# Forgetting attention in a hybrid decoder step: query tiles taken in pairs, the value products of a pair alternating between the two column halves of TensorE

## The chip, the cores and the metric

One NeuronCore of a Trainium2 chip runs one launch of the kernel. The metric is the device time of that launch in microseconds (us). A profiled execution of the kernel before is on hand with its own time beside the span that the profile shows.

## What is computed

The reference is one inference step of a hybrid decoder layer: a combined input projection of 1024 prompt tokens and 32 sample tokens, four parallel head groups (gated DeltaNet, Mamba-2 SSD, forgetting attention "FoX", cross-attention into a memory), an output projection and a LayerNorm. The change is in FoX for the prompt: 8 heads of width 64, 1024 queries and keys, causal, with a cumulative log-forget bias `c`:

```
s = einsum('bqhd,bkhd->bhqk', q, k) * FOX_DH ** -0.5
s = s + cq[..., :, None] - ck[..., None, :]
s = where(k_pos[None, :] <= q_pos[:, None], s, -1e30)
p = softmax(s, axis=-1)
o = einsum('bhqk,bkhd->bqhd', p, v)          # then y_c = o * silu(c_gate)
```

## The kernel before, in words

The kernel is written against a tile framework. Its author writes operations in program order, and a scheduler sets at build time the order in which each engine gets them; on the chip every engine works through its own list in that order and waits on semaphores. So an edit of one function moves instructions of others too, and the order on an engine is read from the built program.

FoX runs in `fox(hp)`, once for each pair of heads hp = 0..3, and in it for both heads of the pair (h2 = 0, 1). A head's queries are cut into eight tiles of 128 (qt = 0..7). Query tile qt needs the keys of blocks 0..qt, in at most two chunks of 512 keys (i = 0, 1). For each chunk:

- scores: matmuls of q1 with k1 and with k2 into a PSUM tile `fs` (lines 586 and 587), a mask matmul on the last block (589), then VectorE adds the bias row `cB`, writes `S` and keeps the row minimum `mn` (590, 593);
- ScalarE takes the exponential in place and sums it into `rs` (597);
- TensorE transposes `S` block by block into the PSUM tile `ft` (helper line 219), ScalarE and VectorE in turn copy it to `P` in SBUF (214, 216);
- value products: for each block of 128 keys one matmul with the value block `vt[:, kt, 64 columns]` as weights and the block of `P` as moving data, accumulated over the blocks in the PSUM tile `fo` (line 605). A value block has 64 columns, so the product fills 64 of the array's 128 columns; `o[64 * h2:64 * h2 + 64]` puts all products of one head into the same column half.

Line 609 multiplies the result into the gate tile `g2`. After both heads the row sums are inverted, transposed (`fr`, `rr`), multiplied in and written to DRAM. A head has 36 key blocks, so all eight heads have 288 value products. Each is fp32 and shows as two records on TensorE, 576 in all.

The tile `vt` (the values of a head pair, 512 KB) is loaded by SyncE's queue (SP) at line 568, two buffers deep; `k1`, `k2`, `q1`, `cB` come by GpSimd's queue (lines 561, 563, 495). SP's queue is in order too: a load that waits for its buffer holds those behind it. `fs` has two PSUM banks, `ft` (shared with `fr`) one, `fo` one.

`run()` weaves the 64 steps of `fox` with 37 steps of the DeltaNet recurrence `gdn()`; the scheduler fills in matmuls of the last input projections (`pj`, line 356) and, once these are used up, of cross-attention (`cs`, `cT`, `co`, `cr`) and of the sample tokens (`zs`, `zo`). Later the SSD part (`by`, line 1372) runs with the output projection (`op`, line 1557). Line 1372 also has weights of 64 columns, and its products go to the two column halves in turn by twos:

```
q, c = 64 * (k % 2), 128 * (k // 2)
nc.tensor.matmul(Y[g][q:q + 64, c:c + 128], lhsT=xdt[:, 4 * g + k, :], rhs=E[:, 4 * g + k, :],
                 start=(k < 2), stop=(n == 0 and k > 1), tile_position=(0, q))
```

Of the kernel before, what the change touches and what calls it, by code (L numbers as in the profile page):

```python
# [10 lines left out]
F32 = mybir.dt.float32  # L11
# [4 lines left out]
AF = mybir.ActivationFunctionType  # L16
ALU = mybir.AluOpType
# [153 lines left out]
class K:  # L171
# [373 lines left out]
    def fox(self, hp):  # L545


        nc, fx = self.nc, self.fx
        vt = fx.tile([128, 8, 128], F32, tag="vt", name="vt", bufs=2)
        g2 = fx.tile([128, T], F32, tag="g2", name="g2", bufs=2)  # L550
# [5 lines left out]
        for h2 in range(2):  # L556
# [16 lines left out]
            for qt in range(8):  # L573
                n = 128 * (qt + 1)
                ch = [(c, min(n, c + 512)) for c in range(0, n, 512)]
                mn = fx.tile([128, 2], F32, tag="mn", name="mn", bufs=3)
                Ss = []
                for i, (c0, c1) in enumerate(ch):
                    p = self.g("fs")
                    S = fx.tile([128, 512], F32, tag="S", name="S", bufs=3)  # L580
                    Ss.append(S)
                    w = c1 - c0

                    w2 = max(w, 256)
                    last = c1 == n
                    nc.tensor.matmul(p[:, :w2], lhsT=q1[:, qt * 128:n], rhs=k1[:, c0:c0 + w2], start=True, stop=False)  # L586
                    nc.tensor.matmul(p[:, :w2], lhsT=q1[:, qt * 128:n], rhs=k2[:, c0:c0 + w2], start=False, stop=not last)  # L587
                    if last:
                        nc.tensor.matmul(p[:, w - 128:w], lhsT=self.identb, rhs=self.foxm, start=False, stop=True)
                    nc.vector.tensor_tensor_reduce(out=S[:, :w], in0=p[:, :w], in1=cB[:, c0:c1], op0=ALU.add, op1=ALU.min,  # L590
                                                   scale=1.0, scalar=3e38, accum_out=mn[:, i:i + 1])
                if len(ch) == 2:
                    nc.vector.tensor_tensor(out=mn[:, 0:1], in0=mn[:, 0:1], in1=mn[:, 1:2], op=ALU.min)
                o = self.g("fo")
                for i, (c0, c1) in enumerate(ch):
                    S, w = Ss[i], c1 - c0
                    nc.scalar.activation(out=S[:, :w], in_=S[:, :w], func=AF.Exp, scale=-1.0, bias=mn[:, 0:1], accum_out=rs[:, qt, h2, i:i + 1])  # L597
# [9 lines left out]
                s = slice(qt * 128, n)  # L607
# [8 lines left out]
        for a in range(2):  # L616
            p = self.g("fr")
            rr = fx.tile([128, 512], F32, tag="S", name="rr", bufs=3)
# [1000 lines left out]
    def run(self):  # L1619
# [4 lines left out]
        with ExitStack() as self.ctx_x:  # L1624
# [46 lines left out]
            t = self.fx.tile([128, 512], F32, tag="P", name="constF", bufs=2)[:, 0:128]  # L1671
# [120 lines left out]
```

## Time and profile before

| | |
|---|---|
| median of 3 runs | 1478.03 us (1476.21 to 1480.02) |
| profiled execution: its own time | 1479.97 us |
| profiled execution: span of the profile | 1478.1 us |
| TensorE (PE) matmul busy | 1373.3 us, 93% |
| PE weight loads (PEld) busy | 1140.2 us, 77% |
| VectorE (DVE) / ScalarE (ACT) / GpSimd (POOL) busy | 829.6 / 499.3 / 440.3 us |
| mean granted TensorE clock | 0.972 of full speed |
| first and last value product of FoX start at | 834.0 and 1186.8 us |

The span runs from the first to the last instruction; the execution's own time is 1.9 us longer. "Busy" of PE counts a matmul from its start to a modelled end, and matmuls are pipelined, so the step from one start to the next says more of its price than its duration. Names such as `fo<-P,vt` read "written tile <- read tiles".

### The profile page before, as it was taken

What the parts mean: (1) busy time and instruction counts of PE and PEld (TensorE: products, weight loads), DVE (VectorE), ACT (ScalarE), POOL (GpSimd) and SP (SyncE); (2) the same over time, 40 slices, a digit from 0 to 9 for tenths busy, and PEclk for the clock granted to TensorE, in tenths of its full rate; (3) what the DMA queues carried; (4) which work ended last, traced back from release to release, by engine and by line L of the source; (5) the groups of instructions that cost most, each with busy time, mean ns of one, the idle gap of its engine ahead of it and who ended that gap; (6) DMA issues with size and microseconds to landing.
All of it is one profiled execution on the core that took longest, in us unless ns stands there. A gap on an engine that the chain in (4) does not pass through costs nothing.

```text
span 1478.1 us, 30323 instructions
## 1 busy us (share of the span) xinstructions
PE 1373.3 (93%) x11222; PEld 1140.2 (77%) x11222; DVE 829.6 (56%) x2149; ACT 499.3 (34%) x1288; POOL 440.3 (30%) x465
## 2 busy tenths in 40 slices
PE   8999999999989998999998899999899978999996
PEld 6898888987777887888887788777676655676764
DVE  4524223364766757452355545777575655866488
ACT  4422222243424343322332333554443320313132
POOL 1445322233524443332201101110120043344446
PEclk9999999999999999999999999999999988999998
DMA  6559898877778886988768444656547465463322
GB/s 241 195 197 377 311 324 312 311 268 272 246 261 299 277 295 234 319 308 298 285 220 209 144 117 119 220 183 178 169 126 212 166 203 191 105 201 89 125 65 106
DMA packets 184477, 324.30 MB, mean 219 GB/s; under 512 B 47177, under 2 KB 110954, under 8 KB 184330
## 3 DMA queue, kind: packets, MB, share of 16 engines
q1 hardware_dynamic: 113744, 241.39, 48.1%
q10 hardware_dynamic: 41930, 59.11, 11.3%
q0 software_dynamic: 28656, 21.88, 5.9%
q8 instruction: 88, 1.44, 0.4%
q14 instruction: 59, 0.48, 0.1%
HBM read 262.23 MB, written 60.01 MB: 218 GB/s over the span
## 4 chain that ended last, share of the span: by engine, by line
PE 42%; DMA 10%; DVE 5%; issue 4%; POOL 2%; ACT 1%; ACTq 0%; SPq 0%; DVEq 0%; POOLq 0%
PE pj L356 13%; PE op L1557 6%; PE fo L605 4%; PE ft L219 2%; PE dA L701 1%; PE fs L586 1%; PE dO L720 1%; DMA bE<-gS 1%; PE co L817 1%; PE fs L587 1%; PE cs L802 1%; DMA ggB<-gS 1%; DMA pg<-in_cache 1%; DMA mr<-mixD 1%; DMA qd<-aD3qd 1%
## 5 line engine op out<-in xcount | busy, mean ns | idle before, releaser
L356 PE MATMUL pj<-xh,wh 128*128 128x352 f32 x1152 | 383.8, 334 | 15.8 <-ACT u L214 8.8
L356 PE MATMUL pj<-xh,wl 128*128 128x352 f32 x1152 | 381.0, 331 | 3.8 <-DVE wl L342 3.8
L356 PE MATMUL pj<-xl,wh 128*128 128x352 f32 x1152 | 380.8, 331 | 0.0
L356 PEld LDWEIGHTS pj<-xh,wh 128*128 128x128 f32 x1152 | 220.4, 192 | 30.5 <-ACT u L214 10.3
L356 PEld LDWEIGHTS pj<-xh,wl 128*128 128x128 f32 x1152 | 221.0, 192 | 11.8 <-issue 6.5
L356 PEld LDWEIGHTS pj<-xl,wh 128*128 128x128 f32 x1152 | 220.4, 191 | 10.7 <-issue 10.0
L1557 PE MATMUL op<-wo,mh 128*128 128x512 f32 x512 | 165.9, 404 | 7.3 <-DVE acc L1563 4.2
L342 POOL TENSOR_TENSOR wl<-wr,wh 128x1024 fp32r<-128x1024 f32 x41 | 97.8, 2386 | 106.5 <-ACT wh L341 101.5
L655 POOL DMA_INDIRECT lf<-in_logf,ix x64 | 68.7, 1073 | 202.5 <-DVE cb L658 151.1
L725 DVE SCALAR_TENSOR_TENSOR Oacc<-Oacc,dmb,dO 128x512 f32<-128x512 f32 x64 | 47.6, 743 | 140.7 <-PE dO L720 132.5
L1557 PEld LDWEIGHTS op<-wo,mh 128*128 128x128 f32 x512 | 97.7, 194 | 37.0 <-issue 8.1
L1557 PE MATMUL op<-wo,ml 128*128 128x512 f32 x256 | 102.9, 404 | 3.2 <-POOL ml L1529 3.1
L900 DVE SCALAR_TENSOR_TENSOR y<-u,cw,y 128x1080 f32<-128x1080 f32 x54 | 79.8, 1477 | 22.7 <-ACT y L898 22.3
L701 PEld LDWEIGHTS dA<-pg,QD 128*32 128x32 f32 x2048 | 60.6, 110 | 40.4 <-issue 27.1
L605 PE MATMUL fo<-P,vt 128*64 128x128 f32 x576 | 83.9, 282 | 6.5 <-DVE P L216 5.6
L701 PE MATMUL dA<-pg,QD 128*32 128x128 f32 x2048 | 81.6, 277 | 8.0 <-DMA pg<-in_cache 4.6
L597 ACT ACTIVATE S<-S,mn 128x512 f32<-128x512 f32 (+2 forms) x96 | 58.6, 611 | 56.5 <-DVE mn L590 35.2
L605 PEld LDWEIGHTS fo<-P,vt 128*64 128x64 f32 x576 | 60.6, 137 | 20.5 <-DVE P L216 7.9
L720 PE MATMUL dO<-pg,dP 128*32 128x512 f32 x512 | 71.0, 598 | 4.7 <-ACT dP L717 4.7
L563 POOL DMA_DIRECT2D k<-kD x16 | 13.2, 837 | 180.1 <-PE fs L587 114.1
L709 ACT ACTIVATE dmb<-dmb 128x1 f32<-128x1 f32 x64 | 18.8, 293 | 130.0 <-DVE dmb L708 113.0
L1557 PEld LDWEIGHTS op<-wo,ml 128*128 128x128 f32 x256 | 49.3, 193 | 17.0 <-POOL ml L1529 4.0
(521 smaller groups left out, 2476.0 us busy)
## 6 DMA issues: line engine op xcount, KB each, us to landing
pg<-in_cache SPq DMA_DIRECT2D x256, 512.0 KB
wr<-in_w_in SPq DMA_DIRECT2D x48, 512.0 KB
k<-kD POOLq DMA_DIRECT2D x16, 512.0 KB, 19.4
wq<-in_w_out SPq DMA_DIRECT2D x16, 512.0 KB
mr<-mixD SPq DMA_DIRECT2D x32, 256.0 KB
xr<-in_xT SPq DMA_DIRECT2D x8, 528.0 KB
gateD<-gt ACTq DMA_DIRECT2D x24, 176.0 KB
mrow<-in_w_mem SPq DMA_DIRECT2D x8, 512.0 KB
```

Of the source, the lines that this page charges most:

```text
L219: self.nc.tensor.transpose(out, in_, self.c("ident", n)[:, :n])
L342: (eng or self.se).tensor_tensor(out=l, in0=r, in1=h.bitcast(F32), op=ALU.subtract)
L356: nc.tensor.matmul(ps[:n], lhsT=w[:, k, :], rhs=x[:, k, s], start=(k == 0 and q == 0), stop=(k == KD - 1 and q == 2))
L597: nc.scalar.activation(out=S[:, :w], in_=S[:, :w], func=AF.Exp, scale=-1.0, bias=mn[:, 0:1], accum_out=rs[:, qt, h2, i:i + 1])
L605: nc.tensor.matmul(o[64 * h2:64 * h2 + 64, 0:128], lhsT=vt[:, kt, 64 * h2:64 * h2 + 64], rhs=P[:, b4 * 128:(b4 + 1) * 128], start=(kt == 0 ...
L655: nc.gpsimd.indirect_dma_start(out=lf, out_offset=None, in_=I["logf"], in_offset=bass.IndirectOffsetOnAxis(ap=ix[:, j:j + 1].bitcast(U32), ...
L701: nc.tensor.matmul(ps[32 * b:32 * b + 32, 0:n], lhsT=QD[:, 4 * gr + b, hp, :], rhs=key(hp, b), start=(hp == 0), stop=(hp == 3), tile_posit ...
L709: nc.scalar.activation(out=mb[:, 1:2], in_=m, func=AF.Exp, scale=-1.0, bias=mb[:, 0:1])
L720: nc.tensor.matmul(po[32 * b:32 * b + 32, :], lhsT=P[:n, 32 * b:32 * b + 32], rhs=value(b), start=True, stop=True, tile_position=(0, 32 * b))
L725: nc.vector.scalar_tensor_tensor(out=O_, in0=O_, scalar=mb[:, 1:2], in1=po, op0=ALU.mult, op1=ALU.add)
L900: nc.vector.scalar_tensor_tensor(out=y, in0=u[:, i:i + CWD], scalar=w[:, i:i + 1], in1=y, op0=ALU.mult, op1=ALU.add)
L1557: nc.tensor.matmul(p[:m], lhsT=l[:, k, :], rhs=W[k][0][:, w, s], start=(k == 0 and q == 0), stop=(k == kn - 1 and q == 2))
```

## The change

Query tiles are taken two at a time, pair (2m, 2m + 1), m = 0..3. The scores, minima and exponentials of both tiles are issued first; then the generator yields, so that the woven parts may come in between; then for each key chunk the transposes and copies of both tiles, and the value products of both. The even tile of the pair goes to column half 0 of one `fo` tile, the odd one to half 1, whatever the head, with an explicit `tile_position`, and block by block the two alternate, odd tile first. Where both tiles' blocks of a chunk number four or fewer, they share one `ft` bank and one copy. Every product of a chunk is issued behind its first one, so a chunk's products start only when both copies are there. Line 609's multiply now reads the half of the tile and writes the half of the head. Buffers: `vt` 2 to 1, `S` 3 to 4, `P` 2 to 3, `mn` 3 to 4.

```diff
-        vt = fx.tile([128, 8, 128], F32, tag="vt", name="vt", bufs=2)
+        vt = fx.tile([128, 8, 128], F32, tag="vt", name="vt", bufs=1)
...
-            for qt in range(8):
...
-                for i, (c0, c1) in enumerate(ch):
-                    S, w = Ss[i], c1 - c0
-                    nc.scalar.activation(out=S[:, :w], ..., accum_out=rs[:, qt, h2, i:i + 1])
-                    P = fx.tile([128, 512], F32, tag="P", name="P", bufs=2)
-                    p = self.g("ft")
-                    for b4 in range(w // 128):
-                        self.tr(p[:, b4 * 128:(b4 + 1) * 128], S[:, b4 * 128:(b4 + 1) * 128])
-                    self.copy(P[:, :w], p[:, :w])
-                    for b4 in range(w // 128):
-                        kt = c0 // 128 + b4
-                        nc.tensor.matmul(o[64 * h2:64 * h2 + 64, 0:128], lhsT=vt[:, kt, 64 * h2:64 * h2 + 64],
-                                         rhs=P[:, b4 * 128:(b4 + 1) * 128], start=(kt == 0), stop=(kt == qt))
+            for m in range(4):
+                pair = (2 * m, 2 * m + 1)
+                mns, Ss = {}, {}
+                for qt in pair:
...
+                    for i, (c0, c1) in enumerate(ch):
+                        S, w = Ss[qt, i], c1 - c0
+                        nc.scalar.activation(out=S[:, :w], ..., accum_out=rs[:, qt, h2, i:i + 1])
+                yield
                 o = self.g("fo")
+                for i in range(len(ch)):
+                    nb = {qt: min(4, qt + 1 - 4 * i) for qt in pair}
+                    P, first = {}, None
+                    for qs in (pair,) if sum(nb.values()) <= 4 else (pair[:1], pair[1:]):
+                        blk = [(qt, b4) for qt in qs for b4 in range(nb[qt])]
+                        Pt = fx.tile([128, 512], F32, tag="P", name="P", bufs=3)
+                        p = self.g("ft")
+                        for j, (qt, b4) in enumerate(blk):
+                            self.tr(p[:, j * 128:(j + 1) * 128], Ss[qt, i][:, b4 * 128:(b4 + 1) * 128])
+                            P[qt, b4] = Pt[:, j * 128:(j + 1) * 128]
+                        self.copy(Pt[:, :128 * len(blk)], p[:, :128 * len(blk)])
+                    for b4 in range(nb[pair[1]]):
+                        kt = 4 * i + b4
+                        for half in (1, 0):
+                            qt = pair[half]
+                            if b4 >= nb[qt]:
+                                continue
+                            with self.tc.issue_after(first.ins) if first else nullcontext():
+                                d = nc.tensor.matmul(o[64 * half:64 * half + 64, 0:128], lhsT=vt[:, kt, 64 * h2:64 * h2 + 64],
+                                                     rhs=P[qt, b4], start=(kt == 0), stop=(kt == qt), tile_position=(0, 64 * half))
+                            first = first or d
-                nc.vector.tensor_tensor(out=g2[r, s], in0=o[r, 0:128], in1=g2[r, s], op=ALU.mult)
+                for half, qt in enumerate(pair):
+                    s = slice(qt * 128, qt * 128 + 128)
+                    nc.vector.tensor_tensor(out=g2[r, s], in0=o[64 * half:64 * half + 64, 0:128], in1=g2[r, s], op=ALU.mult)
                 yield
```

How the built order moves is shown at three places. The first is TensorE's list in the first head, query tiles 2 and 3. Before, each tile's products (`fo`, line 605) stand behind its own transposes:

```order
L219 MATMUL ft_11572<-constG_250,S_11564 128x128 x3
L586 MATMUL fs_11664<-k1_11451,q1_11450 128x512
L587 MATMUL fs_11664<-k2_11452,q1_11450 128x512
L586 MATMUL fs_11669<-k1_11451,q1_11450 128x256
L587 MATMUL fs_11669<-k2_11452,q1_11450 128x256
L589 LDWEIGHTS identb_11220
L589 MATMUL fs_11669<-foxm_11219,identb_11220 128x128
L605 MATMUL fo_11569<-P_11571,vt_11448 64x128 x3
L219 MATMUL ft_11591<-constG_250,S_11583 128x128 x4
L605 MATMUL fo_11588<-P_11590,vt_11448 64x128 x4
```

In the change the same two tiles' seven products stand in one run (now line 620), behind score matmuls of the fourth pair:

```order
L588 MATMUL fs_11787<-k1_11451,q1_11450 128x384
L589 MATMUL fs_11787<-k2_11452,q1_11450 128x384
L591 LDWEIGHTS identb_11220
L591 MATMUL fs_11787<-foxm_11219,identb_11220 128x128
L620 MATMUL fo_11574<-P_11581,vt_11448 64x128
L620 MATMUL fo_11574<-P_11575,vt_11448 64x128
L620 MATMUL fo_11574<-P_11581,vt_11448 64x128
L620 MATMUL fo_11574<-P_11575,vt_11448 64x128
L620 MATMUL fo_11574<-P_11581,vt_11448 64x128
L620 MATMUL fo_11574<-P_11575,vt_11448 64x128
L620 MATMUL fo_11574<-P_11581,vt_11448 64x128
L219 MATMUL ft_11657<-constG_250,S_11627 128x128 x4
```

`P_11581` is the odd tile's copy and `P_11575` the even one's: the two groups became one that alternates. Over all heads the 288 products stand in 96 unbroken groups before and in 52 in the change.

The second place is SP's list at the load of the second head pair's values (`vt<-vD1`). Before, it stands right behind the first loads of the stage:

```order
L568 DMA vt_11448<-vD0_79 128x1024
L569 DMA g2_11449<-gateD8_128 128x1024
L1040 DMA qd_11514<-aD0qd_97 128x512
L1040 DMA Kt_11516<-aD0Kt_99 128x512
L1040 DMA QK_11518<-aD0QK_96 128x512
L568 DMA vt_12367<-vD1_80 128x1024
L569 DMA g2_12368<-gateD9_129 128x1024
```

In the change it stands further down, ahead of a DeltaNet load (`Kp`) and the weights `wq` of the output projection:

```order
L1057 DMA QK_11852<-aD1QK_102 128x512
L1057 DMA Vp_11986<-aD1Vp_106 128x512
L568 DMA vt_12347<-vD1_80 128x1024
L1057 DMA Kp_11988<-aD1Kp_104 128x512
L1515 DMA wq_15588<-in_w_out 128x1024
L1515 DMA wq_15593<-in_w_out 128x1024
L1051 DMA g2_11521<-gateD0_124 128x512
```

The load has moved to where its single buffer comes free, and `Kp` and `wq` now queue behind it. On TensorE's list the first matmul that reads this `Kp` stands some 70 rows behind the first product that reads the new values.

The third place is SP's list at the last values (`vt<-vD3`), in the change:

```order
L1544 DMA mr_15607<-mixD3_139 128x4x128
L568 DMA vt_14051<-vD3_82 128x1024
L1544 DMA mr_15613<-mixD3_139 128x4x128
L864 DMA cmk_15649<-in_cmk 128x1024
L1057 DMA Vp_13879<-aD3Vp_118 128x512
L864 DMA cmk_15655<-in_cmk 128x1024
L1057 DMA Kp_13881<-aD3Kp_116 128x512
```

Before, this load stood ahead of every load from the last DeltaNet head (`aD3`); now it waits behind `mr`, which reads what cross-attention has written (`mixD3`).

On TensorE's list of the change there stand, between the last product of one head pair and the first of the next: at the first handover 41 `pj`, 8 `fr` and 3 `ft` transposes, 8 matmuls of `fs`, 4 `wk`, 4 `sot`, 4 `su`, 16 `lp`; at the second 8 `fr`, 8 `cr`, 3 `cT` and 3 `ft` transposes, 8 of `fs`, 2 `co`, 4 `su`, 28 `lt`, 8 `lp`; at the third 8 `fr`, 3 `ft` and 4 `sot` transposes, 13 of `fs`, 4 `wv`, 4 `wk`, 4 `zs`, 2 `su`.

## Rows read from the trace of the kernel before

**Rows 1.** The page: busy time of each engine over the span, and TensorE's busy tenths and granted clock in 40 slices of 37 us.

```profile
PE 1373.3 (93%) x11222; PEld 1140.2 (77%) x11222; DVE 829.6 (56%) x2149; ACT 499.3 (34%) x1288; POOL 440.3 (30%) x465
...
PE   8999999999989998999998899999899978999996
...
PEclk9999999999999999999999999999999988999998
```

**Rows 2.** Busy time by stretch: from the first value product to 1030 us, and from there to the last one. Columns: stretch, length, then busy us (and instructions) of PE, PEld, DVE, ACT, POOL, granted clock, DMA share, GB/s.

```profile
834.00:1030.00 196.00, 190.46 (x1764) 155.48 (x1763) 123.72 (x393) 89.89 (x273) 16.08 (x20) 1.00 0.52 155
1030.00:1187.00 157.00, 140.97 (x1348) 105.60 (x1346) 96.09 (x337) 64.34 (x205) 16.82 (x19) 0.97 0.52 159
```

**Rows 3.** The chain of waits that ended last, cut to 834 to 1187 us: its shares by line.

```profile
by line: PE fo L605 18.6%; PE ft L219 10.3%; PE pj L356 9.8%; PE fs L586 4.7%; PE co L817 4.0%; PE cs L802 3.9%; PE fs L587 3.8%; DMA qd<-aD3qd 3.5%; DMA A<-aD3A 2.7%; PE su L1147 2.3%; DMA wq<-in_w_out 2.2%; PE wk L1122 2.1%; issue 2.0%; P
```

**Rows 4.** The value products of line 605 as a group: count, and min/median/max of one in ns, with the first and last start.

```profile
L605 PEld LDWEIGHTS fo<-P,vt x576: 132/137/231, 834.0 to 1186.7; 128*64 128x64 f32 x192
L605 PE MATMUL fo<-P,vt x576: 272/273/476, 834.0 to 1186.8; 128*64 128x128 f32 x192
```

**Rows 5.** TensorE's timeline around groups of 2, 4, 6 and 8 records of line 605: start us, length us, what; in brackets the idle time before and who ended it.

```profile
834.04 0.43 PE L605 MATMUL fo<-P,vt 128*64 128x128 f32 x2
834.40 0.44 PE L219 MATMUL ft<-constG,S 128*128 128x128 f32 x2
835.36 0.65 PE L605 MATMUL fo<-P,vt 128*64 128x128 f32 x4 [0.52 <-DVE P L216]
835.94 0.55 PE L219 MATMUL ft<-constG,S 128*128 128x128 f32 x3
...
837.49 0.87 PE L605 MATMUL fo<-P,vt 128*64 128x128 f32 x6
838.29 0.66 PE L219 MATMUL ft<-constG,S 128*128 128x128 f32 x4
839.73 1.09 PE L605 MATMUL fo<-P,vt 128*64 128x128 f32 x8 [0.79 <-DVE P L216]
840.75 0.66 PE L219 MATMUL ft<-constG,S 128*128 128x128 f32 x4
```

**Rows 6.** TensorE's timeline around one run of 16 records of line 1372 (SSD), whose weights have 64 columns too and which uses both column halves.

```profile
1312.21 1.09 PE L1372 MATMUL by<-bE,xdt 128*64 128x128 f32 x16
1313.24 0.43 PE L219 MATMUL yo<-constG,sy 32*128 32x32 f32 x4
```

**Rows 7.** TensorE's waits from 834 to 1187 us, longest first: us in total, times, longest.

```profile
PE su L1147 <- DVE u L1144: 7.1, 1, 7.1
PE fo L605 <- DVE P L216: 5.6, 9, 1.3
PE lt L1075 <- ACT P L1070: 2.2, 1, 2.2
...
PE fo L605 <- ACT P L214: 0.8, 2, 0.5
```

**Rows 8.** TensorE's timeline near 915 and near 1091 us: other work of the stage.

```profile
915.09 0.32 PE L356 MATMUL pj<-xh,wh 128*128 128x352 f32 x1
915.25 0.32 PE L356 MATMUL pj<-xh,wl 128*128 128x352 f32 x1
...
1090.75 0.65 PE L219 MATMUL cr<-constG,drs 128*128 128x128 f32 x4
1091.28 1.16 PE L1122 MATMUL wv<-Vp,DT 128*128 128x128 f32 x8
1092.37 0.43 PE L605 MATMUL fo<-P,vt 128*64 128x128 f32 x2
...
1093.14 0.47 PE L586 MATMUL fs<-k,q 128*128 128x512 f32 x1
1093.46 0.39 PE L587 MATMUL fs<-k,q 128*128 128x512 f32 x1
```

**Rows 9.** Loads of SP's queue in the chain of waits: start us, length us from issue to landing, what (256 KB; 512 KB, one of four issued together; 256 KB).

```profile
869.21 2.64 DMA A<-aD0A
...
930.54 7.71 DMA wq<-in_w_out
...
1102.27 12.53 DMA qd<-aD3qd
```

**Rows 10.** The 16 loads of k by GpSimd's queue (line 563, 512 KB each), from issue to landing.

```profile
DMA to landing us min/median/max: 14.1/19.4/29.7
```

**Rows 11.** SP's timeline: when the values of the third and the fourth head pair were issued.

```profile
970.32 0.42 SPq L568 DMA_DIRECT2D vt<-vD  x1
...
1035.88 0.42 SPq L568 DMA_DIRECT2D vt<-vD  x1
```

**Rows 12.** The instructions of `fo` alone from 1030 to 1187 us: stretch, length, then busy us (and count) of PE, PEld and DVE, granted clock, DMA share, GB/s.

```profile
1030.00:1187.00 157.00, 39.34 (x268) 28.33 (x268) 7.77 (x27) 0.97 0.52 159
```

More of the change, by code (lines that the diff above doesn't have):

```diff
@@ L572, in fox @@
                 nc.vector.memset(rs, 0.0)
-            for qt in range(8):
[L574 to L577, printed above, removed]
-                for i, (c0, c1) in enumerate(ch):
[L579 to L593, printed above, removed]
-                o = self.g("fo")
-                for i, (c0, c1) in enumerate(ch):
-                    S, w = Ss[i], c1 - c0
-                    nc.scalar.activation(out=S[:, :w], in_=S[:, :w], func=AF.Exp, scale=-1.0, bias=mn[:, 0:1], accum_out=rs[:, qt, h2, i:i + 1])
-                    P = fx.tile([128, 512], F32, tag="P", name="P", bufs=2)
-                    p = self.g("ft")
-                    for b4 in range(w // 128):
-                        self.tr(p[:, b4 * 128:(b4 + 1) * 128], S[:, b4 * 128:(b4 + 1) * 128])
-                    self.copy(P[:, :w], p[:, :w])
-                    for b4 in range(w // 128):
-                        kt = c0 // 128 + b4
-                        nc.tensor.matmul(o[64 * h2:64 * h2 + 64, 0:128], lhsT=vt[:, kt, 64 * h2:64 * h2 + 64],
-                                         rhs=P[:, b4 * 128:(b4 + 1) * 128], start=(kt == 0), stop=(kt == qt))
-                s = slice(qt * 128, n)
@@ new lines, in fox @@
+            for m in range(4):
+                pair = (2 * m, 2 * m + 1)
+                mns, Ss = {}, {}
+                for qt in pair:
+                    n = 128 * (qt + 1)
+                    ch = [(c, min(n, c + 512)) for c in range(0, n, 512)]
+                    mn = mns[qt] = fx.tile([128, 2], F32, tag="mn", name="mn", bufs=4)
+                    for i, (c0, c1) in enumerate(ch):
+                        p = self.g("fs")
+                        S = Ss[qt, i] = fx.tile([128, 512], F32, tag="S", name="S", bufs=4)
+                        w = c1 - c0
+                        w2 = max(w, 256)
+                        last = c1 == n
+                        nc.tensor.matmul(p[:, :w2], lhsT=q1[:, qt * 128:n], rhs=k1[:, c0:c0 + w2], start=True, stop=False)
+                        nc.tensor.matmul(p[:, :w2], lhsT=q1[:, qt * 128:n], rhs=k2[:, c0:c0 + w2], start=False, stop=not last)
+                        if last:
+                            nc.tensor.matmul(p[:, w - 128:w], lhsT=self.identb, rhs=self.foxm, start=False, stop=True)
+                        nc.vector.tensor_tensor_reduce(out=S[:, :w], in0=p[:, :w], in1=cB[:, c0:c1], op0=ALU.add, op1=ALU.min,
+                                                       scale=1.0, scalar=3e38, accum_out=mn[:, i:i + 1])
+                    if len(ch) == 2:
+                        nc.vector.tensor_tensor(out=mn[:, 0:1], in0=mn[:, 0:1], in1=mn[:, 1:2], op=ALU.min)
+                    for i, (c0, c1) in enumerate(ch):
+                        S, w = Ss[qt, i], c1 - c0
+                        nc.scalar.activation(out=S[:, :w], in_=S[:, :w], func=AF.Exp, scale=-1.0, bias=mn[:, 0:1], accum_out=rs[:, qt, h2, i:i + 1])
+                yield
+                o = self.g("fo")
+                for i in range(len(ch)):
[19 more added lines that the diff above has]
+                            first = first or d
@@ L617, in fox @@
             p = self.g("fr")
-            rr = fx.tile([128, 512], F32, tag="S", name="rr", bufs=3)
+            rr = fx.tile([128, 512], F32, tag="S", name="rr", bufs=4)
             nc.scalar.copy(rr.rearrange("p (b c) -> p b c", c=64), _bc(ri[:, 4 * a:4 * a + 4, :].rearrange("p b c -> p (b c)"), 64))
@@ L1670, in run @@
             self.identb = self.fx.tile([128, 128], BF16, name="identb")
-            t = self.fx.tile([128, 512], F32, tag="P", name="constF", bufs=2)[:, 0:128]
+            t = self.fx.tile([128, 512], F32, tag="P", name="constF", bufs=3)[:, 0:128]
             nc.sync.dma_start(t, self.I["constF"])
```

## The prediction

> **What bounds the kernel now.** I read the page first. TensorE is busy for 93% of the span, VectorE for 56%, and TensorE's clock is granted at full speed in almost all slices [rows 1]. That is an average, so the question is what bounds the stage in which the value products stand. The busy times by stretch answer it [rows 2]: from 834 to 1030 us TensorE is busy for 190.5 of 196 us, VectorE for 124 and the DMA engines for about half; from 1030 to 1187 us TensorE still has 141 of 157 us. The first stretch is full; the second has 16 us of holes, since the projections that fill in (`pj`) are used up by then. The chain of waits through both says how much of the products is on the path [rows 3]: line 605 has 18.6% of 353 us, 65.7 us, more than any other line.
>
> So TensorE is the bound here and the value products are its largest piece.
>
> **What a product costs.** There are 576 records, two for each of the 288 products, of 273 ns each, and their weight loads take 137 ns [rows 4]. These durations overlap; the price is the step to the next instruction. A group of 2 records holds TensorE for 0.36 us until the next work starts, 4 for 0.58, 6 for 0.80 and 8 for 1.02 [rows 5]. That is 0.11 us for each record and 0.14 us for each group. So now: 576 x 0.11 + 96 groups x 0.14 = 63.4 + 13.4 = 76.8 us.
>
> **What the change makes of it.** The nearest row is in the same trace: line 1372 has the same shape (128 rows, 64 columns, 128 moved) and uses both column halves. A run of 16 of its records takes 1.09 us and holds TensorE for 1.03 [rows 6], where 8 records in one half take 1.09 and 1.02 [rows 5]. Two halves cost what one costs. A pair of query tiles has 4m + 3 products, 2m + 1 of which find a partner; per head that makes 16 couples and 4 singles, for eight heads 128 couples and 32 singles, 160 steps of two records. New price: 160 x 2 x 0.11 + 52 groups x 0.14 = 35.2 + 7.3 = 42.5 us. TensorE is relieved of **34.3 us**: 28.2 from the couples, 6.2 from fewer groups.
>
> The Trainium skill, TensorE: Matmul & The Clock Gate, "Measured speedup vs the span model", gives 2.38x for three column tiles, that is 0.79 of the ideal; at that efficiency two halves would give 1.59x and the 34.3 us would be about 27, an estimate from that page. The run of line 1372 shows the whole factor of two for this shape, so I keep it.
>
> How much of it reaches the end? At most all 34.3. The chain has 65.7 of the 76.8 us on the path, so I take that share: 0.855 x 34.3 = **29.3 us**. The lower bound is nothing, if another chain stands right behind (first rival).
>
> **Waits for the copies.** TensorE waited 6.4 us for `P` at the products [rows 7]. In the new order scores of the next pair stand between a chunk's last transposes and its products, and the exponentials are a whole pair ahead. Between 0 and 6.4 us can go; I take **3**. What is late next there is the second copy of a chunk, because its first product waits for both copies; that wait replaces the two former ones and has more work in front of it. The 16 copies that fall away (80 for 96) are on ScalarE and VectorE, which have room in both stretches [rows 2]; I count nothing for them, nor for the multiply that now reads one half and writes the other: there are still 64 of them on VectorE, and if that cover were gone the one bank of `fo` would make the next group wait for them.
>
> **The single buffer of values.** This is the one wait that the change adds. The values of the third and fourth head pair were issued at 970 and 1036 us [rows 11], long ahead; now each of three loads starts only after the last product of the pair before, and the first new product waits for it. On SP's list `Kp`, `wq`, `mr` or `cmk` stand behind the load and wait with it, but their readers come after the first new products on TensorE's list, so they are not first to be late. Cover is the work between the two products on TensorE's list. At the first handover 41 projections at 0.16 us make 6.6 us, with the rest about 12. At the second 22 transposes at 0.13 make 2.9 us, scores at up to 0.32 about 2, the rest about 2: 7 us. At the third 15 transposes make 2.0, eight `wv` and `wk` products at 0.27 make 2.2, scores about 2.5, the rest under 1: 7.5 us [rows 8]. Together 26.5 us. The load itself (512 KB) has no visible landing; bounds are 2.6 us, a 256 KB load alone on this queue, and 29.7, the longest of the k loads on GpSimd's queue [rows 9, 10]. I take the rows of the same queue in the same stage, 7.7 and 12.5 us: some 8 to 12 us with the release. That leaves nothing at the first handover, 2 at the second and 3 at the third: **5 us** lost. Bounds: 0, and 3 x 29.7 - 26.5 = 63 us.
>
> **Sum.** 1480.0 (the profiled execution's own time) - 29.3 - 3 + 5 = 1452.7 us. The median of the runs shown, 1478.0, is 1.9 us below that execution, so against it: **1451 us**, 1.8% faster. If all bounds fall well, 1478 - 34.3 - 6.4 = 1437; if the handovers cost 15 us and no wait for `P` goes, 1464.
>
> **The rivals.**
>
> *First: the gain stops where the filling work ends.* 268 of the 576 records of the products lie after 1030 us [rows 12], where TensorE already has 16 us of holes and its longest wait, 7.1 us, is on the DeltaNet recurrence [rows 2, 7]. If that recurrence or its loads (`qd`, `A` in the chain [rows 3]) hold the second stretch as it is, only 53% of the gain passes: 15.6 us. 1478 - 15.6 - 3 + 5 = 1464 us, up to 1474. Against it: even there TensorE is busy for 90%, and line 605 stays first in the chain. It decides when the holes after 1030 us grow from 16 to about 30 us.
>
> *Second, on the other side: the values come too late at each handover.* If the loads take as long as k's, the three waits come to 3 x L - 26.5 us, and the gain of 32.3 is used up at L = 19.6 us; k's median is 19.4 [rows 10]. At 25 us the waits are 48.5 and the time is 1494 us. For it: the fourth pair's load falls where other loads of this stage took 12.5 us [rows 9], and behind `mr` on SP's list. Against: no load of SP's queue in the chain took longer than that, and the k loads that could crowd the DMA engines wait for buffers that come free with the scores of a head, ahead of its last products.
>
> *Third: the halves do not overlap,* and every record keeps its 0.11 us. Then only 44 groups go, 6.2 us: 1478 - 6.2 - 3 + 5 = 1474 us. The Trainium skill, TensorE: Matmul & The Clock Gate, "The mechanism", says that a weight load overlaps a running matmul only where the row group differs, and both halves use all 128 rows; by that rule the overlap would be lost. The trace does not bear it out for this shape: 16 records in 1.03 us are 64 ns each, less than half of one weight load [rows 6, 4].
>
> **Chances.** Forecast (1437 to 1464): 0.76. First rival (1464 to 1474): 0.12. Third, with handovers that nearly eat the gain (1474 to 1482): 0.05. Second (above 1482): 0.07. About 0.3% (4.4 us) is what a measurement of this kernel can tell from no change; so faster 0.88, same 0.05, slower 0.07. The range of 8 in 10 takes the forecast's case and the nearer half of the first rival: 1438 to 1470 us.
>
> **What the new profile would show.** Right: the products' runs of 16 records hold TensorE for about 1.03 us; their busy time falls by almost half; the stretch from the first to the last product, 353 us now, is some 27 us shorter, and the work behind it keeps its length. TensorE waits for `vt` for under 8 us in all. The first rival shows as holes after 1030 us with DeltaNet tiles as releasers, the second as a wait of the first product of a head pair on the load of `vt` of over 10 us, three times, the third as runs of 16 that take 2 us. My forecast is wrong if the stage does not shrink by at least 15 us, or if the SSD part behind it, whose order also shifts a little, takes back what the stage gave.

## The result, and the profile after

The changed kernel takes **1439.55 us** (median of 4 runs, 1434.86 to 1439.84) where the kernel before takes 1479.03 on the same chip (4 runs): a ratio of **0.9723** [0.9692, 0.9755]. Forecast were 1451 us, 11 more. The profiled execution is the fastest of the four, 1434.86 us. Ratios stand with their 95% interval and are not exactly the quotients of the medians beside them. Two executions of the later series that took over 1.5% longer than the fastest of the same kernel are left out of medians and ratios.

The page after, the rows that answer to [rows 1], with the line of the products last:

```profile
PE 1329.7 (93%) x11222; PEld 1110.0 (77%) x11222; DVE 823.8 (57%) x2141; ACT 494.7 (35%) x1280; POOL 442.4 (31%) x465
...
PE   7999999999899999999998899898988979999995
...
PEclk9999999999999999999999999899999999999998
...
L620 PE MATMUL fo<-P,vt 128*64 128x128 f32 x576 | 47.9, 288 | 9.6 <-DMA vt<-vD 7.7
```

and the line of the products on the page before:

```profile
L605 PE MATMUL fo<-P,vt 128*64 128x128 f32 x576 | 83.9, 282 | 6.5 <-DVE P L216 5.6
```

TensorE has 43.6 us less to do, at the same 93%. The products (now line 620) are still 576 records, with 47.9 us of busy time for 83.9; most of what they wait for is new, a load of `vt`.

Where the time went is read from three stretches of the span: up to the first value product, from there to the last one (the stage), and behind it. Busy time by stretch (columns as in [rows 2]) of the kernel before, stage and rest:

```profile
834.04:1186.76 352.72, 331.16 (x3109) 261.01 (x3108) 219.81 (x729) 154.19 (x477) 32.90 (x39) 0.99 0.52 157
1186.76:1478.12 291.36, 254.86 (x1425) 184.17 (x1423) 194.71 (x384) 68.48 (x103) 133.15 (x130) 0.93 0.45 138
```

and of the changed kernel, with the two pieces of the stage that answer to [rows 2] first:

```profile
826.00:1030.00 204.00, 187.76 (x1897) 155.21 (x1897) 133.05 (x416) 96.38 (x293) 19.14 (x24) 0.95 0.53 155
1030.00:1152.00 122.00, 109.06 (x1194) 82.61 (x1196) 83.54 (x288) 54.06 (x178) 14.76 (x20) 0.97 0.62 193
...
826.93:1152.46 325.53, 296.35 (x3095) 237.87 (x3093) 216.33 (x706) 149.96 (x469) 34.20 (x44) 0.96 0.56 170
1152.46:1433.10 280.64, 249.58 (x1439) 181.95 (x1436) 193.55 (x400) 68.09 (x104) 135.96 (x125) 0.97 0.49 145
```

The stage is 27.2 us shorter, the part behind it 10.7, the part ahead of it 7.1. In the stage TensorE's busy time fell by 34.8 us, but its idle time (length less busy) rose from 21.6 to 29.2, and the granted clock fell from 0.99 to 0.96. The 16 us that [rows 2] had as holes behind 1030 us did not grow (12.9 now, in 122 us); new holes stand ahead of it, 16.2 us where there were 5.5. Behind the stage idle time fell from 36.5 to 31.1 us and the clock rose from 0.93 to 0.97.

TensorE's longest waits in the stage after (us in total, times, longest); they answer to [rows 7]:

```profile
PE fo L620 <- DMA vt<-vD: 7.7, 1, 7.7
PE fr L219 <- DVE g L640: 5.0, 1, 5.0
PE l2p L1123 <- ACT DT L1118: 3.0, 1, 3.0
PE su L1164 <- DVE u L1161: 2.7, 1, 2.7
PE fo L620 <- DVE P L216: 1.9, 2, 1.4
```

Of the three handovers of `vt` from one head pair to the next one waits, the second. SP's timeline has the load's issue at 993.01, TensorE's has the first product at 1004.17, 11.2 us later:

```profile
993.01 0.41 SPq L568 DMA_DIRECT2D vt<-vD  x1
```

```profile
1004.17 1.09 PE L620 MATMUL fo<-P,vt 128*64 128x128 f32 x6 [7.71 <-DMA vt<-vD]
```

### The profile page after: what moved, and what is told of

It reads as the page before. It is cut to its first block, busy times and chain, and to the rows that moved or that the text cites. A ratio compares the mean times of both kernels' runs of the same rounds, so it can differ in the third digit from the quotient of the medians.

```text
span 1433.1 us, 30270 instructions
## 1 busy us (share of the span) xinstructions
PE 1329.7 (93%) x11222; PEld 1110.0 (77%) x11222; DVE 823.8 (57%) x2141; ACT 494.7 (35%) x1280; POOL 442.4 (31%) x465
## 5 line engine op out<-in xcount | busy, mean ns | idle before, releaser
L356 PEld LDWEIGHTS pj<-xh,wh 128*128 128x128 f32 x1152 | 219.1, 191 | 28.1 <-issue 10.7
L356 PEld LDWEIGHTS pj<-xh,wl 128*128 128x128 f32 x1152 | 219.8, 191 | 11.5 <-issue 6.3
L1574 PE MATMUL op<-wo,mh 128*128 128x512 f32 x512 | 162.9, 398 | 3.1 <-DVE lr L1587 1.6
L737 PE MATMUL dO<-pg,dP 128*32 128x512 f32 x512 | 71.8, 605 | 4.1 <-ACT dP L734 3.9
L592 DVE CUSTOM_DVE_ANT_0 S<-fs,cB 128x512 f32<-128x512 f32 (+2 forms) x96 | 52.5, 551 | 19.9 <-PE ft L219 15.0
L1193 POOL TENSOR_TENSOR rb<-ra,constG 128x4 f32<-128x4 f32 (+1 forms) x9 | 8.7, 971 | 156.5 <-DVE ra L1192 156.5
L620 PE MATMUL fo<-P,vt 128*64 128x128 f32 x576 | 47.9, 288 | 9.6 <-DMA vt<-vD 7.7
```

The source lines that it names most:

```text
L356: nc.tensor.matmul(ps[:n], lhsT=w[:, k, :], rhs=x[:, k, s], start=(k == 0 and q == 0), stop=(k == KD - 1 and q == 2))
L620: d = nc.tensor.matmul(o[64 * half:64 * half + 64, 0:128], lhsT=vt[:, kt, 64 * h2:64 * h2 + 64], rhs=P[qt, b4], start=(kt == 0), stop=(kt ...
L737: nc.tensor.matmul(po[32 * b:32 * b + 32, :], lhsT=P[:n, 32 * b:32 * b + 32], rhs=value(b), start=True, stop=True, tile_position=(0, 32 * b))
L1574: nc.tensor.matmul(p[:m], lhsT=l[:, k, :], rhs=W[k][0][:, w, s], start=(k == 0 and q == 0), stop=(k == kn - 1 and q == 2))
```

## The experiments

In all of them "price of the products" is the sum, over the 576 records, of the steps from a record's start to the start of TensorE's next matmul, taken from the trace: 78.0 us before, 44.3 after (the prediction worked out 76.8 and 42.5). Code is cut at `...`.

### First four: one edit each, the scheduler sets the order anew

*One half.* Both tiles of a pair on one column half, side by side in the bank of `fo` (the multiply behind them reads them there):

```
-  d = nc.tensor.matmul(o[64 * half:64 * half + 64, 0:128], ..., start=(kt == 0), stop=(kt == qt), tile_position=(0, 64 * half))
+  d = nc.tensor.matmul(o[0:64, 128 * half:128 * half + 128], ..., start=(kt == 0 and half == 1), stop=(kt == qt and half == 1), tile_position=(0, 0))
```

> The change, but the odd tile's products go to the same column half as the even one's (other columns of the same fo tile): pairing, alternation, buffers and copies stay, no two neighbouring products can overlap. Theory 1 (the stage's gain is the overlap of the two halves): a run of 16 records holds TensorE for about 1.9 us instead of 1.0, the price of the products rises from 42.5 to about 70 us, the stretch from the first to the last product from 325.6 to about 350 us, and the time to 1462 to 1468 us. Theory 2 (the gain is the pairing: fewer groups, exponentials a pair ahead, fewer waits): the time stays within 5 us of 1440. On the 10.7 us gained behind the last product: if they come from the order in which that part now stands, this kernel has them too (about 281 us from the last product to the end); if they come from the overlap, it has the 291 us of before.

*Half of the values early.*

```
-  vt = fx.tile([128, 8, 128], F32, tag="vt", name="vt", bufs=1)
+  vt = [fx.tile([128, 4, 128], F32, tag=f"vt{j}", name="vt", bufs=2 - j) for j in range(2)]
```

Each half has a load of its own. To make room, `P` has two buffers instead of three.

> The change, with the values in two tiles of four key blocks, the first of them two buffers deep (the second one deep), and P two deep instead of three to make room. The first blocks of a new head pair can then be loaded early. Theory 1 (the one wait of the products for the values, 7.7 us, is on the path): the wait goes and the time falls by 4 to 8 us, to about 1433. Rival (TensorE would have waited there for something else, or waits for P instead): within 3 us of 1439.5.

*Four then four.* The loop over the halves moves outside the loop over the blocks:

```
-  for b4 in range(nb[pair[1]]):
-      ...
-      for half in (1, 0):
-          qt = pair[half]
+  for half in (1, 0):
+      qt = pair[half]
+      for b4 in range(nb[qt]):
+          ...
```

> The change, but within a chunk all products of the odd tile come first and then all of the even one's: up to four products in one half, then up to four in the other. Theory 1a (each half takes its own products from a queue that looks past those of the other half): same as the change, 1440 us, runs of 16 records hold TensorE for 1.0 us. Theory 1b (matmuls are handed out in order, one half's products hold back the other's): only neighbours at the seam overlap, runs of 16 take about 1.8 us, the time is as with one half, 1460 to 1466 us.

*The kernel before with one buffer of values* (`vt`: `bufs=2` to `bufs=1`, nothing else).

> The kernel before with the values one buffer deep and nothing else changed. Theory 1 (a single buffer costs a wait at a handover, 5 us in the forecast and 7.7 us in the new trace): 1480 to 1487 us. Rival (the order finds cover for it, as at two of the three handovers of the new trace): within 3 us of 1478.

Measured (ratios to the kernel before, 18 runs, median 1478.1 us): one half 1.0079 [1.0043, 1.0115]; half of the values early 0.9914 [0.9882, 0.9945]; four then four 0.9888 [0.9852, 0.9924]; before with one buffer 0.9923 [0.9892, 0.9953]. The first, the second and the fourth lie outside what any theory gave. The third's time, 1466.8 us, is just above its theory 1b, but its price of products, 56.8 us, lies between those of alternating halves and of one half (73.4). The kernel before came out 0.8% faster with a buffer less, and in its profile no product waits for `vt`. The second edit says nothing of the load alone, since with two buffers of `P` the products wait 18.5 us for `P`.

The profiles give a reason for the misses: the stages are 360.7, 330.5, 336.8 and 356.9 us, but the part behind them, whose instructions no edit touched, is 297.4, 306.8, 299.9 and 286.2. Each edit changed the order that the scheduler wrote for all engines: at 2169 of the 8438 places of TensorE's list one half has another operation or other tiles than the changed kernel. These runs mix the edit with its order, so the next ones hold the order.

### The order held

At the end of the build every engine's instructions are chained in a given order, by dependencies that fix the place in the list and add no wait on the chip:

```
+    for i in np.frombuffer(zlib.decompress(base64.b64decode(_ORDER)), dtype=np.int16):
+        if i >= 0 and prev is not None:
+            tc.add_manual_dep(L[i], prev.name, info, reason="order")
+        prev = L[i] if i >= 0 else None
```

`_ORDER` has the instructions of the traced program, engine by engine. Every engine's list of one half below is then, in the built program, that of the changed kernel, instruction for instruction, but for the half.

*One half, in the order of the changed kernel* (same edit as one half above):

> The changed kernel with one edit: both tiles' products go to the same column half and write beside each other in the group's bank, so that no product overlaps another. Every engine issues every instruction in exactly the order of the changed kernel; only the half differs. Theory 1 (the gain between the first and the last product is the overlap of the two halves alone): the price of the products goes from 44.3 us to 73.4 as in the run with one half in its own order, all of it on TensorE's path, so the stretch is 325.5 + 29 = 355 us (352 to 357), the part behind it stays at 281 (278 to 284), and the time is 1439.6 + 29 = 1468 us (1464 to 1472). Theory 2 (what the one-half run lost came from the overlap and not from the order it was given): 1487 us with its own order, so 1483 to 1490 here too. Theory 3 (the order that the pairing leads to is worth it, the overlap little): 1440 to 1446 us.

*The changed kernel, its other work in the order of before*, and *the kernel before, its other work in the order of after* (only the chain of instructions outside `fox` is given):

> The changed kernel, program unchanged, but each engine issues everything that is not of the scores, exponentials and products of FoX (7508 of TensorE's instructions) in the order in which the kernel before issues it among itself; where the FoX instructions stand between them is left free. Theory 1 (the 11 us gained behind the last product, 291.4 to 280.6, come from the order in which the other work stands there): 291 us behind the last product, stretch of the products 326, 1446 to 1454 us. Theory 2 (they are chance of the profiled executions or follow from the shorter products): 281 us there and 1437 to 1442 us.

> The kernel before, its program unchanged, but each engine issues everything that is not of FoX's scores, exponentials and products in the order in which the changed kernel issues it among itself. Theory 1 (the order of the other work is worth the 11 us behind the last product): 281 us there, the stretch of the products 353 as before, 1464 to 1470 us. Theory 2 (it is not the order): 291 us there and 1476 to 1481 us.

*Four then four, in the order of the changed kernel* (same edit as above):

> The changed kernel with the products of a chunk in another order: those of one tile (half 1), then those of the other (half 0), instead of in turn; 128 of TensorE's 8438 instructions trade places, everything else on every engine stands as in the changed kernel. Theory 1 (only products next to each other on different halves overlap; the price of the products is 56.8 us as in the run with this order of the products and a schedule of its own, 12.5 above the 44.3): stretch 338 us, behind it 281, 1450 to 1454 us. Theory 2 (the order of the other work was what cost that run its time): 1440 to 1445 us. Theory 3 (the order of the products costs all of what that run lost against the changed kernel): 1464 to 1469 us.

Measured (kernel before in these runs 1484.0 us, 16 runs): one half 1450.3 us, 0.9762 [0.9709, 0.9816]; changed kernel with the other work as before 1473.9 (10 runs, 1471 to 1492), 0.9986 [0.9942, 1.0030]; before with the other work as after 1469.3, 0.9913 [0.9878, 0.9948]; four then four 1450.4 (4 runs: 1440, 1443, 1458, 1461), 0.9794 [0.9721, 0.9867]. One half lies between theories 1 and 3, the second kernel beyond both of its theories, the third where theory 1 put it. Four then four is not decided: its median is that of theory 1, but two of its runs lie at theory 2 and two above theory 1, and the profile, of the fastest run, has a stage of 332.4 us where theory 1 had 338 and the changed kernel has 325.5.

The overlap itself is as the prediction read it. The same run of 16 records with the instruction behind it, from TensorE's timelines of the changed kernel, of one half and of four then four, all three in one order:

```profile
877.58 1.09 PE L620 MATMUL fo<-P,vt 128*64 128x128 f32 x16
878.61 0.55 PE L219 MATMUL ft<-constG,S 128*128 128x128 f32 x3
```

```profile
880.07 1.96 PE L620 MATMUL fo<-P,vt 128*64 128x128 f32 x16
881.96 0.55 PE L219 MATMUL ft<-constG,S 128*128 128x128 f32 x3
```

```profile
878.20 1.58 PE L618 MATMUL fo<-P,vt 128*64 128x128 f32 x16
879.71 0.55 PE L219 MATMUL ft<-constG,S 128*128 128x128 f32 x3
```

From start to start 1.03, 1.89 and 1.51 us; the price of all products is 44.3, 71.8 and 56.7. So alternating halves take 27.5 us off the price of the products. The time did not follow in full. Stage and rest of one half in that order:

```profile
825.64:1163.18 337.54, 320.57 (x3093) 264.24 (x3093) 213.36 (x708) 151.16 (x469) 34.23 (x44) 0.97 0.55 166
1163.18:1449.14 285.96, 252.92 (x1438) 183.33 (x1436) 193.63 (x397) 68.03 (x103) 135.33 (x125) 0.96 0.49 140
```

Its stage is 12.0 us longer than that of the changed kernel, not 27.5: busy time is 24.2 us more, idle time 12.2 less (17.0 for 29.2). So of the 27.5 us that alternating saves on the products, 12.0 shorten the stage, 12.2 turn into idle time, and 3.3 go to the rest of TensorE's work there, which takes longer, at a granted clock of 0.96 for 0.97. The waits of one half, against the list above:

```profile
PE fr L219 <- DVE g L640: 3.5, 1, 3.5
PE l2p L1123 <- ACT DT L1118: 2.6, 1, 2.6
PE su L1164 <- DVE u L1161: 2.0, 1, 2.0
PE fo L620 <- DVE P L216: 2.0, 2, 1.4
...
PE fo L620 <- DMA vt<-vD: 1.2, 1, 1.2
```

With slower products the load of `vt` is nearly in time (1.2 us of wait for 7.7), and the wait of `fr` for VectorE is shorter. That one is for the most part a load too. VectorE's timeline, then TensorE's, in the changed kernel where `fr` waits 5.0 us:

```profile
1081.91 0.27 DVE L1099 MEMSET D<- 64x256 f32 x1
1086.25 1.17 DVE L1082 TENSOR_TENSOR AL<-A,constG 32x128 f32<-32x128 f32 x4 [4.07 <-DMA A<-aD3A]
...
1089.16 0.68 DVE L640 TENSOR_TENSOR g<-fr,g 128x512 f32<-128x512 f32 x1
```

```profile
1083.77 1.11 PE L1139 MATMUL wv<-Vp,DT 128*128 128x128 f32 x8
1089.90 0.90 PE L219 MATMUL fr<-constG,rr 128*128 128x128 f32 x3 [5.02 <-DVE g L640]
```

Line 640 stands on VectorE's list behind line 1082, which waits 4.07 us for the load of `A`, and some 2.9 us of VectorE's work lie between the start of the one and that of the other. The wait's name is `g`; most of it is a DeltaNet load on SP's queue.

The pair of kernels with the other work's order exchanged shows what the scheduler's order is worth. The kernel before gains some 0.9% by that order alone (1469.3 us for 1484.0). Its stage and rest:

```profile
827.98:1182.41 354.43, 330.65 (x3101) 261.10 (x3100) 215.21 (x725) 155.32 (x477) 34.12 (x44) 0.98 0.54 156
1182.41:1465.96 283.55, 251.59 (x1433) 181.88 (x1431) 192.98 (x388) 67.93 (x103) 136.22 (x125) 0.96 0.49 142
```

Its stage is no shorter than before (354.4 us for 352.7); the part behind it is 7.8 us shorter and nearly that of the changed kernel. The changed kernel in the order of before loses its whole gain, all of it behind the stage:

```profile
824.90:1144.30 319.40, 289.38 (x2964) 231.37 (x2964) 207.84 (x679) 147.56 (x456) 30.46 (x36) 0.96 0.54 157
1144.30:1469.40 325.10, 276.28 (x1568) 198.28 (x1565) 207.12 (x426) 70.86 (x116) 135.57 (x133) 0.89 0.45 141
```

325.1 us with 48.8 idle and a granted clock of 0.89. The order of before was made for a longer stage; some work that stood in it now comes behind it (1568 records for 1439).

### Once more on one chip, and a version without the wait

*The changed kernel again; one half in the order of the changed kernel again; two blocks of the values early, with all else in the order of the changed kernel:*

```
-  vt = fx.tile([128, 8, 128], F32, tag="vt", name="vt", bufs=1)
+  vt = [fx.tile([128, n, 128], F32, tag=f"vt{n}", name="vt", bufs=b) for n, b in ((2, 2), (6, 1))]
```

> The changed kernel as it is, to stand beside the next two on one chip. It was 0.9723 of the kernel before (0.9692 to 0.9755), and the same again is expected; between the first and the last product 322 to 329 us, 277 to 285 behind it. Before the first product the earlier profiled execution took 826.9 us where that of the kernel before took 834.0, with the same instructions in the same order: if that is chance, this one may lie anywhere from 822 to 834.

> The changed kernel with both tiles' products on one half, every engine's instructions in the order of the changed kernel, run again beside it. Theory 1 (TensorE's waits give back part of what the overlap saves: the products cost 27.5 us more, the waits and the stretches at the lower clock 13 less): 1.007 to 1.012 times the changed kernel of the same call, 10 to 17 us. Theory 2 (the overlap is worth its full price, and the first run of this kernel was a lucky one): 1.017 to 1.020 times, 25 to 29 us. Theory 3 (at a fixed order the overlap is worth nothing that can be told): within 0.3%.

> The changed kernel with the values in two tiles: blocks 0 and 1 double buffered and loaded ahead, blocks 2 to 7 single as now, so that a pair's first group of products (query tiles 0 and 1) never waits for the load; four more loads on SP, every other instruction in the order of the changed kernel. Theory 1 (the wait for the values, 7.7 us in the profiled execution of the changed kernel, is on the path and nothing takes its place, since the next group comes 10 us later): no such wait, 6 to 9 us less than the changed kernel of the same call, 0.994 to 0.996 of it. Theory 2 (the wait moves to the next one, the exponentials or the groups of reciprocals on VectorE): within 3 us of it.

Measured: 1438.7 us, 0.9732 [0.9702, 0.9761]; 1449.9, 0.9800 [0.9760, 0.9841]; 1432.5, 0.9679 [0.9638, 0.9719]. Stage of the changed kernel, then of one half:

```profile
831.83:1158.42 326.59, 297.47 (x3094) 238.99 (x3093) 216.78 (x706) 150.29 (x469) 34.20 (x44) 0.95 0.57 170
```

```profile
833.51:1170.97 337.46, 319.12 (x3094) 263.24 (x3093) 213.32 (x708) 151.05 (x469) 34.18 (x44) 0.98 0.56 166
```

The stages repeat to about 1 us: 326.6 for 325.5, and 337.5 for 337.5, and of the two one half again waits less for `vt` (3.5 us for 9.0). By the medians the overlap is worth **11.2 us** here at the order of the changed kernel (1.0078 times), by the ratios 0.7%, and the intervals of the two ratios just touch. Theory 1 fits; the full price, 25 us and more, is refuted. The part ahead of the stage took 831.8, 833.5 and 834.3 us in these three, 822 to 834 over all profiled executions, so the 7.1 us there in the first comparison are chance.

With two blocks early the wait for `vt` is gone (9.0 us in the changed kernel beside it, 0.3 now), the stage is 322.4 us for 326.6, and the median is 6.2 us lower. That is at the lower end of theory 1, but the two intervals overlap, so a gain over the changed kernel is likely and not established. The stage gains half of the 8.7 us. Some 3 us of the rest turned up as a new wait: VectorE stands 6.1 us for the load of `A` of the third head, and `su` then waits for VectorE. VectorE's timeline, then TensorE's:

```profile
1015.10 1.17 DVE L1082 TENSOR_TENSOR AL<-A,constG 32x128 f32<-32x128 f32 x4 [6.11 <-DMA A<-aD2A]
```

```profile
1017.37 0.80 PE L1164 MATMUL su<-u,Kt 128*128 128x128 f32 x2 [2.84 <-DVE u L1161]
```

### The fourth corner

*The changed kernel in the order that one half had been given:*

> The fourth corner of the square of half and order: the changed kernel, its program unchanged, with every engine's instructions in the order that the one-half kernel had been given for itself (1.0079 of the kernel before, 360.7 us from the first to the last product, 297.4 behind it). Theory 1 (at a fixed order the overlap saves 27 to 29 us of products and TensorE's waits take some 60% of that back, as in the order of the changed kernel): the stretch about 349 us, 297 behind it, ratio to the kernel before 0.998 to 1.002. Theory 2 (waits took it back there because that order leaves other engines late; in an order made for slow products there are as many waits already, and the full price comes through): the stretch 332 us, ratio 0.987 to 0.990. Theory 3 (an order that is wrong for the overlap gives nothing): within 0.3% of the one-half kernel, 1.005 to 1.011.

Measured: 1478.7 us (10 runs), 0.9992 [0.9961, 1.0023], as theory 1 expected, though it put the waits a little low: the stage is 352.3 us, not 349, and behind it are 302.6. Stage and rest of one half, then the stage of the changed kernel, both in that order:

```profile
822.38:1183.11 360.73, 327.27 (x3097) 268.12 (x3097) 214.36 (x714) 151.16 (x469) 34.22 (x44) 0.96 0.56 155
1183.11:1480.51 297.40, 256.54 (x1434) 186.56 (x1432) 194.90 (x391) 68.38 (x103) 140.29 (x125) 0.95 0.47 135
```

```profile
828.12:1180.40 352.28, 307.25 (x3097) 245.77 (x3097) 217.67 (x714) 150.44 (x469) 34.10 (x44) 0.93 0.57 159
```

Busy 20.0 us less, idle 11.5 more: 8.5 us shorter. The price of the products fell by 28.5 us here (73.4 to 44.9), so 8.5 of them went to the rest of TensorE's work, which took longer at a granted clock of 0.93 for 0.96. The waits that the shorter products lengthen are only in part those of the first order: that for `vt` grew by 2.2 us (1.0 to 3.2), but that for a load of `dq` by 4.1 (1.2 to 5.3). With this the square is full (ratio to the kernel before):

| | order of one half | order of the changed kernel |
|---|---|---|
| one half | 1.0079 [1.0043, 1.0115] | 0.9762 [0.9709, 0.9816]; 0.9800 [0.9760, 0.9841] |
| halves in turn | 0.9992 [0.9961, 1.0023] | 0.9723 [0.9692, 0.9755]; 0.9732 [0.9702, 0.9761] |

Downwards, the overlap, is 0.4 to 0.9%, some 6 to 13 us; across, the order, is 2.6 to 3.2%, some 38 to 47 us. Within the intervals the one does not depend on the other. The chain itself shows no price: one half is chained in the right column and halves in turn in the left one, so a price would enter the two overlaps with opposite signs, and these come out at 0.4 to 0.7% and at 0.9%, apart by less than their intervals.

## Why the prediction was right, and where it was not

**The result.** Faster, and inside the range, 1.6 us above its low end. The cause that was forecast, the overlap, is there, but it gives only some 10 of the 40 us; the rest comes with an order that the prediction gave no price. Too much credit for the overlap and none for the order nearly cancelled, and that the number came so close is luck.

**The price of the products: right.** Forecast 76.8 to 42.5 us, a relief of 34.3; measured 78.0 to 44.3, 33.7. Of this 27.5 is the overlap (71.8 to 44.3 at one order; 28.2 forecast) and 6.2 the fewer and longer groups (78.0 to 71.8; 6.2 forecast). Runs of 16 take 1.03 us as line 1372 did [rows 6]. The Trainium skill's 2.38x for three column tiles (TensorE: Matmul & The Clock Gate, "Measured speedup vs the span model"), taken for two halves, would have given an estimate of about 27 us in place of 33.7; the row of the same shape was the better guide.

**The third rival (no overlap): refuted,** by 1.03 against 1.89 us for the same run. The rule behind it (the Trainium skill, TensorE: Matmul & The Clock Gate, "The mechanism": weight loads overlap only where the row group differs) does not hold here: both halves use the same 128 rows. Even on one half a record took 0.12 us, less than the 0.137 of its weight load [rows 4], so that loads run beside other records' work there too.

**The share that reaches the end, 0.855: wrong.** This is the step that failed: of 34.3 us, 29.3 were to reach the end. The prediction took the products' share in the chain of waits [rows 3] for the share of a saving. With the order held, of 27.5 us 12.0 come through in one order (0.44), and in the other 8.5 of 28.5 (0.30; price 73.4 to 44.9). The chain says what is on the path now, not what stands behind it. Behind it, in the order of the changed kernel, stood SP's loads (`vt`, `A`) and VectorE's list; in the other order loads too, of `dq` and `vt`. The waits that are named make up some 8 of the 12.2 us of idle time in the first order (`vt` 6.5, `fr` 1.5), the rest is spread over small ones. A second part, 3.3 and 8.5 us, went to TensorE's other work at the lower granted clock. The waits are the first rival's mechanism at another place: it looked for holes behind 1030 us, and they came ahead of it.

**The stage, 27 us shorter: hit, for another reason.** The prediction held the order for a given and let the saving pass through it. In truth the order is the larger part. From profile to profile the stage goes from 352.7 us (before) to 360.7 by pairing on one half in the order made for it, to 337.5 by the order of the changed kernel, and to 325.5 by the overlap: +8.0, -23.2 and -12.0. For the whole time the same steps are +0.8% (1.0079), -2.8 (1.0079 to 0.9800) and -0.7 (0.9800 to 0.9732), together the 2.7% that were measured, some +12, -41 and -10 us. How a change of the half leads the scheduler to another order is not seen in a trace.

**The work behind the stage "keeps its length": wrong.** 291.4 to 280.6 us, and 282.8 in the second profile of the changed kernel: about the 11 us by which the forecast was too high. It is the order there: the kernel before with that order has 283.5. Of the 10.7 us, 5.4 are idle time of TensorE and 5.3 busy time, at a granted clock of 0.97 for 0.93. The prediction read the 9s of [rows 1] as full speed; they stand for any clock from 0.9 on, and this part had 0.93. The prediction named this place, as a risk of a loss only.

**Waits for `P`: right in sign.** 6.4 us [rows 7] to 1.9; forecast 3 less, measured 4.5.

**The single buffer of values: about right in sum, not handover by handover.** Forecast 0, 2 and 3 us, under 8 in all; measured 0, 7.7 and 0, and 9.0 in the second profile. From issue to first product the second handover took 11.2 us, within the 8 to 12 assumed. In the kernel before the single buffer, with the order that came with it, costs no time (0.9923). The second rival fell with this.

**What stays open:** which single moves in the order make the some 40 us. The orders differ in many places (2169 on TensorE alone), and no run undid them one by one.

## What to carry to other kernels

When a scheduler writes the order, an edit is two changes, its own and that of the order, and the second can be the larger: hold the order of all engines fixed before crediting the edit, and fill the square of edit and order. A line's share in the chain of waits is not the share of a saving that comes through (0.855 against 0.44 and 0.30 here). What comes through is read from what the other engines and queues would then be late with, and a wait on VectorE may be a load that its list is stuck behind.

## What the runs showed of the hardware

Two column halves overlap even if the list does not alternate, but only near the seam, where the list passes from one half to the other. In the run of four then four shown above (eight records for each half, one half after the other on the list) the trace has five starts, the first step 160 ns and the others 109; then, 6 ns after the fifth, at 878.689 us, a second row of starts sets in, and for some 0.3 us two rows run side by side, each with the same steps. The trace names no half; read so, the second half starts while three records ahead of it on the list have not. On one half, in the same order, no product starts less than 109 ns behind the one before it, which speaks for this reading. It gives the 0.38 us between 1.89 and 1.51. The price of all products falls by 15 of the 27.5 us that alternating saves.

Much idle time and a low clock come together, but not in step: behind the stage the granted clock is 0.97 with 31.1 us idle (the changed kernel), 0.93 with 36.5 (before) and 0.89 with 48.8 (the changed kernel in the order of before), yet 0.95 with 40.9 (one half in its own order). Which brings which was not tried.
